# One hybrid attention and convolution trunk: normalized operands made in staggered pairs, and the rest of the gated branch handed out along the last projection

## The chip, the cores and the metric

The kernel runs on one core of a Trainium2 chip. The metric is the device time of one execution in microseconds (us). Engines are named as the profile names them: PE is TensorE, DVE is VectorE, ACT is ScalarE, POOL is GpSimd and SP is SyncE, which issues the DMAs. Every engine works through its own queue in order and waits on semaphores that the others raise.

## The reference, cut to what matters

A sequence of 256 rows of width 2048 runs through two layers and a final RMSNorm, all in float32:

```
hn = rmsnorm(x, norm_g[0])                     # layer 0: forgetting attention, 16 heads of 128
q, k, v, gate, f = split(hn @ fox_w_in)
c = cumsum(log_sigmoid(f + b_f))
p = softmax(q k^T * scale + c_q - c_k, causal)
h = x + ((p v) * silu(gate)) @ fox_w_out

hn = rmsnorm(h, norm_g[1])                     # layer 1: causal Conformer convolution
a, b, gate = split(hn @ conv_w_in + b_in)
u = causal depthwise conv(a * sigmoid(b), 31 taps) + dw_b
y = silu(layernorm(u)) * silu(gate)
out = rmsnorm(h + y @ conv_w_out, final_norm_g)
```

## The kernel before

**Matmuls in three passes.** Every float32 operand is cut in two fp32r numbers: an upper half (the value copied to fp32r by ScalarE, line L100) and a lower half (the value minus its upper half, line L101, on VectorE or GpSimd as the code says). A product is upper x upper, upper x lower, lower x upper. Weights come from HBM in 1 MB tiles (`raw`, three buffers), are cut into `hi` and `lo` (three buffers each), and TensorE takes 48 matmuls of 256 columns from a tile (24 of 512 columns in the value projection and in the last one). A new `hi` can be written when TensorE is through with the tile three before it.

**Order.** TensorE's order is written out by hand. Behind it runs a counter, `now`: a k-row of a 512-wide tile is one step (12 matmuls of 256 columns). `at(n, f)` issues f once the counter has moved on by n, in front of the next k-row (`step`). `line` with `put` is a second list, for VectorE's long work in the convolution: each entry has a length in steps, and entries are issued as the counter passes the sum of the lengths. In layer 0 the tile framework chooses the order on ScalarE, VectorE and GpSimd by the place in the program at which an instruction is issued; from L710 to the first quarter of the last projection the order on these three is also the order of the program.

**Forget sums.** In the first head group the forget gate's log is made on GpSimd in small operations (L494 to L516) into `lfn`. `forget_sums`, issued by `at(18.5, ...)` in L654, sums it along the sequence by two matmuls (`pc`, L524); ScalarE copies the result (`chi`, L527), VectorE builds `cc` (L528 to L531), and GpSimd multiplies `cc` by a head's selector into `la` and `rbh` (L558 to L561). A head's score needs them in its last two matmuls (L566, L567).

**Layer 1.** The first two blocks of 128 channels (b and a of each) are projected from the unnormalized h, and the norm's row scale is applied to the result (`scaled`, L919 to L922). All later blocks use normalized operands `nh` and `nl`, which `normed` (L785) makes for two k-rows at a time: VectorE multiplies h by the row scales into a PSUM tile `n` (L789), ScalarE makes the upper half `nh` (L281), VectorE the lower half `nl` (L282), row after row. Two pairs are put on the line by `norm1_rows`, six more by block 0 (L926), ahead of that block's convolution. Then VectorE runs 31 taps per channel (L814). After the first channel block `mean_shift` (L847) takes a mean by two matmuls on TensorE from its result `dall`; it is issued 12 steps after block 1. At the end of each later pair of channels ScalarE and GpSimd add up sums (L866 to L871).

**The gated branch.** After the LayerNorm, `gated` (L982) makes the normalized, silu'd pair of channels in PSUM, and `gated2` (L994) multiplies it by the gate `sg` and cuts it into the halves `y1a` (channels 0 to 7 of 16) or `y1b` (8 to 15). `y1b` has the place of `nh` in memory, so it cannot be written before the last gate projection has read `nh`. L1014 to L1018 issue the last four pairs at one place ahead of the last projection, whose first quarter (`po`, L244 to L246) takes `y1b` from its ninth k-row on. The weights of that quarter are four tiles from `feed_tiles` (L688), here called c0 to c3, with lower halves from GpSimd in two pieces each; the next quarter's tiles are here called d0 to d3.

Of the kernel before, what the change touches and what calls it, by code (L numbers as in the profile page):

```python
# [8 lines left out]
F32 = mybir.dt.float32  # L9
F32R = mybir.dt.float32r  # L10
AF = mybir.ActivationFunctionType
ALU = mybir.AluOpType

P = 128
D = 2048
S = 256
# [18 lines left out]
def tile_hybrid_trunk(  # L35
# [112 lines left out]
    def feed_tiles(wv, c0, width, engs, order=None):  # L148

        n = KT * width // 2048  # L150
        first = len(feed["specs"])
        feed["specs"] += [(wv, c0, width, (order or range(n))[g], engs) for g in range(n)]
        return first
# [22 lines left out]
    def at(step, fn):  # L176
        agenda.append((now[0] + step, fn))
        agenda.sort(key=lambda e: e[0])
# [438 lines left out]
    for pos, hg in enumerate(ORDER):  # L617

        kT = [
            ph.tile([P, 4, n], dt, name=f"k{i}_{hg}", tag=f"k{i}", bufs=1)  # L620
            for i, (n, dt) in enumerate(((S, F32R), (S, F32R), (P, F32)))
        ]
        qT = [
            ph.tile([P, 4, P], dt, name=f"q{i}_{hg}", tag=f"q{i}", bufs=1) for i, dt in enumerate((F32R, F32R, F32))
        ]
        ps = k_banks if pos == 0 else proj_t(w_fin, D + hg * 512, 512, tiles(ah), tiles(al), VE)

        def qk_evict(dst, ps, scale):
            for b in range(2):
                bs = slice(2 * b, 2 * b + 2)  # L630
                pv = ps[b].rearrange("p (a t) -> p a t", a=2)
                e = ph.tile([P, 2, P], F32, tag="ge", name=f"e{n_stream[0]}_{b}")
                for m, part in enumerate((dst[2][:, bs, :], e)):
                    ts = slice(m * P, (m + 1) * P)
                    nc.vector.scalar_tensor_tensor(
                        part, pv[:, :, ts], scale, rb[:, :, ts].broadcast_to([P, 2, P]), op0=ALU.mult, op1=ALU.mult
                    )
                if dst is kT:
                    for m, part in enumerate((dst[2][:, bs, :], e)):
                        ts = slice(m * P, (m + 1) * P)  # L640
                        split(kT[0][:, bs, ts], kT[1][:, bs, ts], part, nc.gpsimd)
                else:
                    split(qT[0][:, bs, :], qT[1][:, bs, :], e, nc.gpsimd)

        if pos == 0:
            at(8, lambda: row_scales(r0, rb[:, 0, :], "l0"))
            at(11, lambda: qk_evict(kT, k_banks, 1.0))
        else:
            qk_evict(kT, ps, 1.0)
        ps = proj_t(w_fin, hg * 512, 512, tiles(ah), tiles(al), VE, 4 if pos == 0 else 1, made=() if pos else q_made)  # L650
        qk_evict(qT, ps, -float(P) ** -0.5)
        sil = gate_group(hg)
        if pos == 0:
            at(18.5, forget_sums)  # L654
        vN = [
            ph.tile([P, 512], dt, tag=f"v{i}", name=f"v{i}_{hg}", bufs=1) for i, dt in enumerate((F32R, F32R, F32))
        ]
        ps = [psj.tile([P, 512], F32, tag="pj", name=f"pv{hg}_{m}") for m in range(2)]
        for kt, hv, lv in stream(w_fin, 2 * D + hg * 512, 512, VE):
            for m in range(2):  # L660
                products_n(ps[m], kt, hv, lv, tiles(ah), tiles(al), m, kt == 0, kt == KT - 1)
        nc.scalar.activation(vN[0], ps[0], AF.Copy, scale=r0[:, 0:1])
        nc.vector.scalar_tensor_tensor(
            vN[1], ps[0], r0[:, 0:1], vN[0].bitcast(F32), op0=ALU.mult, op1=ALU.subtract
        )
        nc.scalar.activation(vN[2], ps[1], AF.Copy, scale=r0[:, 1:2])
        dist, t0 = 3 if pos < 3 else 2, 0 if pos else 6
        for j in range(4):
            attend(4 * hg + j, qT, kT, vN, sil, t0 + dist * j, t0 + dist * j + 5, t0 + dist * j + 8)
# [15 lines left out]
        a_first[c0] = feed_tiles(w_cin, c0, width, GE if c0 == P else engs)  # L685
    for c in range(4):
        g_first[c] = feed_tiles(w_cin, 2 * D + c * 512, 512, GE)
    cout0 = feed_tiles(w_cout, 0, 512, GE * 2)  # L688

    def residual_add(n, b, ps):  # L690
        kp = slice(4 * n + 2 * b, 4 * n + 2 * b + 2)
# [86 lines left out]
    def norm1_rows(r1):  # L778
        rows = bank_rows(kept_bank("rbk"), 0, r1, "l1")
        put(0.3, lambda: nc.vector.tensor_copy(rb1, rows))  # L780
        for kp in range(2):
            put(0.96, lambda kp=kp: normed(kp, rows))
        kept["rows"] = rows

    def normed(kp, rows):  # L785

        t = bank(f"n{kp}").rearrange("p (a t) -> p a t", a=2)
        ks = slice(2 * kp, 2 * kp + 2)
        nc.vector.tensor_tensor(t, hT[:, ks, :], rows.broadcast_to([P, 2, S]), op=ALU.mult)  # L789
        for i in range(2):  # L790
            split_act(2 * kp + i, 1, nh, nl, t[:, i, :])

    negs = ph.tile([P, S], F32, name="negs", bufs=1)
    accd = ph.tile([P, 2, S], F32, name="accd", bufs=1)
# [98 lines left out]
    def conv_block(c0, width):  # L893
        ct, n = c0 // P, width // P
        normal = ct >= 2
        h, l = (nh, nl) if normal else (ah, al)
        pb = proj_t(w_cin, D + c0, width, tiles(h), tiles(l), None, first=b_first[c0])[0]
        sig = ph.tile([P, 2, S], F32, tag="sig", name=f"sig{ct}", bufs=2)
        if normal:

            at(0.4, lambda: [sigmoid(ct + i, sig[:, i, :], pb[:, i * S : (i + 1) * S]) for i in range(n)])
        pa = proj_t(w_cin, c0, width, tiles(h), tiles(l), None, first=a_first[c0])[0]

        def start():
            bks = [gated_input(ct + i, pa[:, i * S : (i + 1) * S], sig[:, i, :]) for i in range(n)]

            rest = line[:]
            line.clear()
            if n == 1:
                conv_alone(ct, bks[0])  # L910
            else:
                conv_pair(ct, bks)
            line[4:4] = [e for e in rest if e in sums]
            line.extend(e for e in rest if e not in sums)

        if not normal:
            rows = rb1[:, 0, :]

            def scaled():  # L919
                nc.vector.tensor_tensor(sig[:, 0, :], pb[:, 0:S], rows, op=ALU.mult)  # L920
                nc.vector.tensor_tensor(pa[:, 0:S], pa[:, 0:S], rows, op=ALU.mult)
                sigmoid(ct, sig[:, 0, :], sig[:, 0, :])  # L922

            if ct == 0:
                put(2 * HALF, scaled)
                for kp in range(2, KT // 2):  # L926
                    put(0.96, lambda kp=kp: normed(kp, kept["rows"]))
                put(HALF, start)
            else:

                line.insert(min(4, len(line)), (2 * HALF, scaled))
                put(HALF, start)
            return
        put(2 * HALF, start)
# [77 lines left out]
        pump(True)  # L1012
        agenda.pop(0)[1]()
    yb = big.tile([P, 2, HK, S], F32R, tag="B1", name="y1b")  # L1014
    for cp in (4, 5, 6, 7):
        if cp == 7:
            gated(7)
        gated2(cp)  # L1018

    def yh(kt):  # L1020
        return (ya if kt < HK else yb)[:, 0, kt % HK, :]
# [125 lines left out]
```

## Time and profile before

| | us |
|---|---|
| median of 3 runs (lowest, highest) | 897.37 (897.13, 897.63) |
| profiled execution, its own time | 897.78 |
| its span (first to last instruction) | 895.8 |
| PE busy | 876.0 (98%) |
| DVE, ACT, POOL busy | 566.9, 421.8, 381.5 |
| mean granted clock of PE | 0.993 |

The span runs from the first to the last instruction of the profiled execution; the other 1.98 us of its time lie around it. Matmuls overlap, so a busy share of 98% says that PE seldom stands, not that it could do no more. The granted clock is a share of 2.4 GHz; PE runs at that or at half of it.

### The profile page before, as it was taken

Reading aid. Unit: us, or ns where it says so; the run is one execution under the profiler, and the core shown is the slowest. Engines: PE = TensorE matmul, PEld = TensorE weight load, DVE = VectorE, ACT = ScalarE, POOL = GpSimd, SP = SyncE. Lnnn points to the kernel's source line nnn. Section 1 sums busy time; section 2 is a strip of 40 time slices with the busy share of each in tenths; the row PEclk is TensorE's granted clock in tenths of the full one; section 3 lists DMA queues with packets and bytes.
Section 4 is the critical chain, followed back from the end, with each engine's and each line's share of the span. In section 5 each row is a group of like instructions: output and inputs, shape, how many; then the busy total and the mean of one; then the engine's idle time right before and its main releaser. Section 6 shows DMA issues by size and latency. Waiting matters only on the chain.

```text
span 895.8 us, 15928 instructions
## 1 busy us (share of the span) xinstructions
PE 876.0 (98%) x6652; PEld 845.7 (94%) x6652; DVE 566.9 (63%) x1035; ACT 421.8 (47%) x558; POOL 381.5 (43%) x237
## 2 busy tenths in 40 slices
PE   9999999999999999999999988999999999999996
PEld 9999899989999999989999978999999999988886
DVE  5764455446544564446656559999999993628641
ACT  5743355345434553356444463444443355756531
POOL 4130954103410231103100248799798998755110
PEclk9999999999999999999999998999999999999998
DMA  9887987976577998954455446445555556456522
GB/s 290 231 236 152 181 155 142 181 194 180 141 187 171 173 161 171 184 198 160 149 189 152 142 142 199 164 158 186 189 188 188 188 168 208 145 187 232 178 109 94
DMA packets 99499, 157.71 MB, mean 176 GB/s; under 512 B 2676, under 2 KB 40676, under 8 KB 99300
## 3 DMA queue, kind: packets, MB, share of 16 engines
q1 hardware_dynamic: 99092, 155.63, 64.3%
q8 instruction: 52, 0.85, 0.4%
q10 hardware_dynamic: 336, 1.07, 0.3%
q14 instruction: 19, 0.16, 0.0%
HBM read 154.59 MB, written 2.10 MB: 175 GB/s over the span
## 4 chain that ended last, share of the span: by engine, by line
PE 89%; DVE 3%; POOL 3%; ACT 2%; issue 2%; POOLq 0%; DVEq 0%; ACTq 0%
PE pt L216 68%; PE po L246 3%; PE po L245 3%; PE po L244 3%; PE pv L245 2%; PE pv L246 2%; PE pv L244 2%; DVE acc L814 1%; ACT hi L100 1%; DVE nl L282 1%; ACT nh L281 1%; PE sc L564 1%; POOL fg L500 1%; POOL fg L502 1%; PE warm L326 1%
## 5 line engine op out<-in xcount | busy, mean ns | idle before, releaser
L100 ACT ACTIVATE hi<-raw 128x2048 fp32r<-128x2048 f32 (+2 forms) x185 | 270.5, 1485 | 307.5 <-PE pt L216 196.8
L101 DVE TENSOR_TENSOR lo<-raw,hi 128x2048 fp32r<-128x2048 f32 (+1 forms) x132 | 217.6, 1673 | 186.5 <-ACT hi L100 186.3
L101 POOL TENSOR_TENSOR lo<-raw,hi 128x2048 fp32r<-128x2048 f32 (+1 forms) x53 | 227.9, 4313 | 61.0 <-ACT hi L100 61.0
L216 PE MATMUL pt<-ah,hi 128*128 128x256 f32 x768 | 219.6, 286 | 0.0
L216 PE MATMUL pt<-ah,lo 128*128 128x256 f32 x768 | 217.3, 283 | 0.0
L216 PE MATMUL pt<-al,hi 128*128 128x256 f32 x768 | 217.3, 283 | 0.0
L216 PE MATMUL pt<-nh,lo 128*128 128x256 f32 x704 | 200.5, 285 | 4.1 <-POOL lo L101 4.1
L216 PE MATMUL pt<-nh,hi 128*128 128x256 f32 x704 | 201.0, 286 | 0.2 <-ACT hi L100 0.2
L216 PE MATMUL pt<-nl,hi 128*128 128x256 f32 x704 | 200.3, 285 | 0.0
L814 DVE SCALAR_TENSOR_TENSOR acc<-u,dwT,acc 128x256 f32<-128x256 f32 x478 | 188.3, 474 | 0.0
L216 PEld LDWEIGHTS pt<-al,hi 128*128 128x128 f32 x768 | 147.4, 192 | 0.1
L216 PEld LDWEIGHTS pt<-ah,hi 128*128 128x128 f32 x768 | 147.3, 192 | 0.1
L216 PEld LDWEIGHTS pt<-ah,lo 128*128 128x128 f32 x768 | 147.3, 192 | 0.0
L216 PEld LDWEIGHTS pt<-nh,lo 128*128 128x128 f32 x704 | 136.4, 194 | 4.3 <-POOL lo L101 4.3
L216 PEld LDWEIGHTS pt<-nh,hi 128*128 128x128 f32 x704 | 136.5, 194 | 0.5 <-ACT hi L100 0.4
L216 PEld LDWEIGHTS pt<-nl,hi 128*128 128x128 f32 x704 | 136.4, 194 | 0.1
L216 PE MATMUL pt<-yh,hi 128*128 128x256 f32 x256 | 73.3, 286 | 0.0
L216 PE MATMUL pt<-yl,hi 128*128 128x256 f32 x256 | 72.5, 283 | 0.6 <-POOL yl L101 0.6
L216 PE MATMUL pt<-yh,lo 128*128 128x256 f32 x256 | 72.4, 283 | 0.0
L558 POOL CAST la<-ones 64x256 fp32r<-64x256 f32 x16 | 8.5, 529 | 136.0 <-PE sc L567 135.9
L244 PE MATMUL pv<-hi,ah 128*128 128x512 f32 x128 | 50.0, 390 | 0.0
L216 PEld LDWEIGHTS pt<-yl,hi 128*128 128x128 f32 x256 | 49.1, 192 | 0.8 <-POOL yl L101 0.8
(260 smaller groups left out, 1221.1 us busy)
## 6 DMA issues: line engine op xcount, KB each, us to landing
raw<-in_fox_w_in_dram SPq DMA_DIRECT2D x56, 1024.0 KB, 7.6
raw<-in_conv_w_in_dram SPq DMA_DIRECT2D x48, 1024.0 KB, 5.2
raw<-in_fox_w_out_dram SPq DMA_DIRECT2D x16, 1024.0 KB, 5.1
raw<-in_conv_w_out_dram SPq DMA_DIRECT2D x16, 1024.0 KB, 5.1
raw<-in_fox_w_in_dram SPq DMA_DIRECT2D x4, 1056.0 KB, 7.3
rawk<-in_fox_w_in_dram SPq DMA_DIRECT2D x4, 512.0 KB, 10.9
xn<-in_x_dram SPq DMA_DIRECT2D x3, 512.0 KB, 11.2
rawk<-in_fox_w_in_dram SPq DMA_DIRECT2D x4, 256.0 KB, 5.5
```

The costliest lines, as they stand in the source:

```text
L100: nc.scalar.activation(dst_hi, src, AF.Copy)
L101: lo_eng.tensor_tensor(dst_lo, src, dst_hi.bitcast(F32), op=ALU.subtract)
L216: nc.tensor.matmul(ps[nt // 2][:, (nt % 2) * S : (nt % 2 + 1) * S], w[:, nt * P : (nt + 1) * P], a(kt), start=(kt == 0 and i == 0 and nt % ...
L244: nc.tensor.matmul(ps, ah(kt)[:, ms], hv, start=first, stop=False)
L245: nc.tensor.matmul(ps, al(kt)[:, ms], hv, start=False, stop=False)
L246: nc.tensor.matmul(ps, ah(kt)[:, ms], lv, start=False, stop=last)
L281: nc.scalar.activation(hi_t[:, kt, :], src, AF.Copy, scale=gcol)
L282: nc.vector.scalar_tensor_tensor(lo_t[:, kt, :], src, gcol, hi_t[:, kt, :].bitcast(F32), op0=ALU.mult, op1=ALU.subtract)
L326: nc.tensor.matmul(warm[:, 0:P], ones, ones, start=True, stop=True)
L500: g.tensor_tensor(e, base, e, op=ALU.pow)
L502: g.tensor_tensor(s2, s2, neg1, op=ALU.pow)
L814: nc.vector.scalar_tensor_tensor(acc, src, w, acc, op0=ALU.mult, op1=ALU.add)
```

## The change

- `forget_sums` is issued one step later (19.5 instead of 18.5).
- `normed` takes a pair in two calls: one makes `n` and both `nh` of pair kp, and the next one, after the `n` and `nh` of pair kp + 1, makes both `nl` of pair kp. There are nine calls instead of eight, three of them ahead of block 0's own.
- The lower halves of c0 to c3 come from VectorE instead of GpSimd, in two pieces as before.
- In front of the last projection the third tile's halves are issued first (`feed_make(cout0 + 2)`), and the last four pairs of the gated branch are issued at steps 0.5, 1.5, 2.5 (`gated2` 4 to 6), 3.5 (`gated` 7) and 6 (`gated2` 7) of it.

```diff
@@ -651,7 +651,7 @@
         qk_evict(qT, ps, -float(P) ** -0.5)
         sil = gate_group(hg)
         if pos == 0:
-            at(18.5, forget_sums)
+            at(19.5, forget_sums)
         vN = [
             ph.tile([P, 512], dt, tag=f"v{i}", name=f"v{i}_{hg}", bufs=1) for i, dt in enumerate((F32R, F32R, F32))
         ]
@@ -685,7 +685,7 @@
         a_first[c0] = feed_tiles(w_cin, c0, width, GE if c0 == P else engs)
     for c in range(4):
         g_first[c] = feed_tiles(w_cin, 2 * D + c * 512, 512, GE)
-    cout0 = feed_tiles(w_cout, 0, 512, GE * 2)
+    cout0 = feed_tiles(w_cout, 0, 512, VE * 2)
 
     def residual_add(n, b, ps):
         kp = slice(4 * n + 2 * b, 4 * n + 2 * b + 2)
@@ -778,17 +778,27 @@
     def norm1_rows(r1):
         rows = bank_rows(kept_bank("rbk"), 0, r1, "l1")
         put(0.3, lambda: nc.vector.tensor_copy(rb1, rows))
-        for kp in range(2):
-            put(0.96, lambda kp=kp: normed(kp, rows))
         kept["rows"] = rows
-
-    def normed(kp, rows):
-
-        t = bank(f"n{kp}").rearrange("p (a t) -> p a t", a=2)
-        ks = slice(2 * kp, 2 * kp + 2)
-        nc.vector.tensor_tensor(t, hT[:, ks, :], rows.broadcast_to([P, 2, S]), op=ALU.mult)
-        for i in range(2):
-            split_act(2 * kp + i, 1, nh, nl, t[:, i, :])
+        for kp in range(3):
+            put(0.96, lambda kp=kp: normed(kp))
+
+    def normed(kp):
+
+        if kp < KT // 2:
+            t = kept[kp] = bank(f"n{kp}").rearrange("p (a t) -> p a t", a=2)
+            nc.vector.tensor_tensor(
+                t, hT[:, 2 * kp : 2 * kp + 2, :], kept["rows"].broadcast_to([P, 2, S]), op=ALU.mult
+            )
+            for i in range(2):
+                kt = 2 * kp + i
+                nc.scalar.activation(nh[:, kt, :], t[:, i, :], AF.Copy, scale=gT[:, KT + kt : KT + kt + 1])
+        if kp:
+            for i in range(2):
+                kt = 2 * kp - 2 + i
+                nc.vector.scalar_tensor_tensor(
+                    nl[:, kt, :], kept[kp - 1][:, i, :], gT[:, KT + kt : KT + kt + 1], nh[:, kt, :].bitcast(F32),
+                    op0=ALU.mult, op1=ALU.subtract,
+                )
 
     negs = ph.tile([P, S], F32, name="negs", bufs=1)
     accd = ph.tile([P, 2, S], F32, name="accd", bufs=1)
@@ -923,8 +933,8 @@
 
             if ct == 0:
                 put(2 * HALF, scaled)
-                for kp in range(2, KT // 2):
-                    put(0.96, lambda kp=kp: normed(kp, kept["rows"]))
+                for kp in range(3, KT // 2 + 1):
+                    put(0.96, lambda kp=kp: normed(kp))
                 put(HALF, start)
             else:
 
@@ -1012,10 +1022,11 @@
         pump(True)
         agenda.pop(0)[1]()
     yb = big.tile([P, 2, HK, S], F32R, tag="B1", name="y1b")
-    for cp in (4, 5, 6, 7):
-        if cp == 7:
-            gated(7)
-        gated2(cp)
+    feed_make(cout0 + 2)
+    for i, cp in enumerate((4, 5, 6)):
+        at(0.5 + i, lambda cp=cp: gated2(cp))
+    at(3.5, lambda: gated(7))
+    at(6, lambda: gated2(7))
 
     def yh(kt):
         return (ya if kt < HK else yb)[:, 0, kt % HK, :]
```

The names in the rows below are the program's tiles with a buffer number. On VectorE, where the normalized operands are made: `n` is the product of a pair, `nl` its lower halves, `dwT` the taps' weights, `sig` and `pt` block 0's scaling. Before, in the first rows from `n`:

```order
L789 TENSOR_TENSOR n_5465<-hT,rbk 128x512
L282 SCALAR_TENSOR_TENSOR nl_5350<-n_5465,gT,nh_5349 128x256 x2
L762 COPY dwT<-pd 128x496
L789 TENSOR_TENSOR n_5489<-hT,rbk 128x512
L282 SCALAR_TENSOR_TENSOR nl_5350<-n_5489,gT,nh_5349 128x256 x2
L920 TENSOR_TENSOR sig_5419<-pt_0_5355,rb_5336 128x256
L921 TENSOR_TENSOR pt_0_5420<-pt_0_5420,rb_5336 128x256
L789 TENSOR_TENSOR n_5520<-hT,rbk 128x512
```

Here each pair's `nl` follows its own `n`. The same place of VectorE now:

```order
L789 TENSOR_TENSOR n_5465<-hT,rbk 128x512
L762 COPY dwT<-pd 128x496
L789 TENSOR_TENSOR n_5487<-hT,rbk 128x512
L798 SCALAR_TENSOR_TENSOR nl_5350<-n_5465,gT,nh_5349 128x256 x2
L789 TENSOR_TENSOR n_5509<-hT,rbk 128x512
L798 SCALAR_TENSOR_TENSOR nl_5350<-n_5487,gT,nh_5349 128x256 x2
L930 TENSOR_TENSOR sig_5419<-pt_0_5355,rb_5336 128x256
L931 TENSOR_TENSOR pt_0_5420<-pt_0_5420,rb_5336 128x256
L789 TENSOR_TENSOR n_5536<-hT,rbk 128x512
```

Each pair's `nl` now stands behind the next pair's `n`. On ScalarE and then on VectorE, around the forget sums (`hi_1458` and `lo_1459` are the halves of the second k projection's fourth tile, `hi_1370` and `lo_1371` those of its third):

```order
 L100 ACTIVATE hi_1370<-raw_1368 128x2048
 L666 ACTIVATE v_3_1053<-pv_1_1055,r_l_499 128x512
+L100 ACTIVATE hi_1458<-raw_1456 128x2048
 L527 ACTIVATE chi<-pc 128x256
-L100 ACTIVATE hi_1458<-raw_1456 128x2048
 L580 ACT_TABLE_LOAD
```

The upper half now stands ahead of `chi`. VectorE at the same place:

```order
 L101 TENSOR_TENSOR lo_1371<-raw_1368,hi_1370 128x2048
+L101 TENSOR_TENSOR lo_1459<-raw_1456,hi_1458 128x2048
 L528 COPY cc<-chi 128x256
 L531 TENSOR_TENSOR cc<-pc,chi 32x256 x2
-L101 TENSOR_TENSOR lo_1459<-raw_1456,hi_1458 128x2048
 L574 ISA e_1333,nm_1334<-sc_1326,cmask 128x256
```

The lower half now stands ahead of `cc`. On ScalarE, from the last gate projection's silu (`sg`) into the last projection: `hi_8834` and `hi_8866` are c2 and c3, `hi_8969` and `hi_9017` are d0 and d1, `t_8815` is the last pair. Before:

```order
L942 ACTIVATE sg<-pt_1_8543,par 128x256 x2
L100 ACTIVATE y1b<-t_8587 128x512
L100 ACTIVATE y1b<-t_8626 128x512
L100 ACTIVATE y1b<-t_8659 128x512
L990 ACTIVATE t_8815<-t_8815,par 128x256 x2
L100 ACTIVATE y1b<-t_8815 128x512
L100 ACTIVATE hi_8834<-raw_8832 128x1024 x2
L100 ACTIVATE hi_8866<-raw_8864 128x1024 x2
L100 ACTIVATE hi_8969<-raw_8967 128x512 x4
L100 ACTIVATE hi_9017<-raw_9015 128x512 x4
```

All four `y1b` stand ahead of c2, c3, d0 and d1. Now (`hi_8808` and `hi_8863` are c2 and c3, `t_8852` is the last pair):

```order
L952 ACTIVATE sg<-pt_1_8534,par 128x256 x2
L100 ACTIVATE hi_8808<-raw_8806 128x1024 x2
L100 ACTIVATE y1b<-t_8599 128x512
L100 ACTIVATE y1b<-t_8638 128x512
L100 ACTIVATE y1b<-t_8671 128x512
L1000 ACTIVATE t_8852<-t_8852,par 128x256 x2
L100 ACTIVATE hi_8863<-raw_8861 128x1024 x2
L100 ACTIVATE hi_8969<-raw_8967 128x512 x4
L100 ACTIVATE hi_9017<-raw_9015 128x512
L100 ACTIVATE y1b<-t_8852 128x512
L100 ACTIVATE hi_9017<-raw_9015 128x512 x3
```

The third tile now stands ahead of the gated pairs, the fourth ahead of the last pair's `y1b`, and that `y1b` behind d0 and one piece of d1.

## Rows read from the trace of the kernel before

**Rows 1.** Who waited for whom, TensorE over the whole span: total, times, longest

```profile
PE pt L216 <- POOL lo L101: 4.1, 1, 4.1
PE pm L847 <- DVE dall L838: 3.5, 1, 3.5
...
PE lnb L775 <- ACT dg_mr L774: 0.3, 1, 0.3
```

**Rows 2.** TensorE in time: start, duration (us), line, operation, idle before <- releaser

```profile
525.69 0.28 PE L216 MATMUL pt<-nh,hi 128*128 128x256 f32 x1
525.81 0.28 PE L216 MATMUL pt<-nl,hi 128*128 128x256 f32 x1
...
536.39 0.58 PE L216 MATMUL pt<-nh,lo 128*128 128x256 f32 x1 [4.09 <-POOL lo L101]
...
552.71 0.96 PE L847 MATMUL pm<-dall,ones 128*128 128x256 f32 x2 [3.52 <-DVE dall L838]
```

**Rows 3.** Stretches: busy us of PE, PEld, DVE, ACT, POOL; granted clock, DMA

```profile
553.00:556.50 3.50, 3.50 (x17) 3.37 (x16) 3.50 (x10) 0.10 (x1) 3.50 (x1) 0.52 0.93 299
...
800.00:850.00 50.00, 48.28 (x223) 39.29 (x222) 32.85 (x38) 30.36 (x54) 16.16 (x8) 1.00 0.58 195
```

**Rows 4.** Groups, 504 to 560 us: busy, mean ns | idle before, releaser

```profile
L282 DVE SCALAR_TENSOR_TENSOR nl<-n,gT,nh 128x256 fp32r<-128x256 f32 x16 | 7.7, 484 | 11.0 <-ACT nh L281 11.0
L281 ACT ACTIVATE nh<-n,gT 128x256 fp32r<-128x256 f32 x16 | 7.6, 473 | 12.8 <-DVE n L789 8.3 <-DVE nl L282 4.5
L789 DVE TENSOR_TENSOR n<-hT,rbk 128x512 f32<-128x512 f32 x8 | 5.5, 685 | 0.0
```

**Rows 5.** Timeline of VectorE in the same stretch

```profile
511.43 0.69 DVE L789 TENSOR_TENSOR n<-hT,rbk 128x512 f32<-128x512 f32 x1
...
514.15 0.67 DVE L762 COPY dwT<-pd 128x496 f32<-128x496 f32 x1
...
536.31 0.08 DVE L801 MEMSET u<- 128x30 f32 x1
...
540.76 9.09 DVE L814 SCALAR_TENSOR_TENSOR acc<-u,dwT,acc 128x256 f32<-128x256 f32 x23
```

**Rows 6.** Timeline of ScalarE and of GpSimd in the same stretch

```profile
518.78 1.28 ACT L808 ACT_TABLE_LOAD   x1
...
529.84 1.90 ACT L100 ACTIVATE hi<-raw 128x2048 fp32r<-128x2048 f32 x1
...
531.82 4.51 POOL L101 TENSOR_TENSOR lo<-raw,hi 128x2048 fp32r<-128x2048 f32 x1 [8.35 <-ACT hi L100]
```

**Rows 7.** Timeline of four engines around the forget sums

```profile
111.51 1.13 PE L524 MATMUL pc<-tri,lfn 128*128 128x256 f32 x4 [0.80 <-POOL lfn L516]
...
117.29 0.36 PE L566 MATMUL sc<-rbh,la 128*128 128x256 f32 x1
...
113.98 1.91 ACT L100 ACTIVATE hi<-raw 128x2048 fp32r<-128x2048 f32 x1 [0.92 <-PE pt L216]
...
108.33 2.29 DVE L101 TENSOR_TENSOR lo<-raw,hi 128x2048 fp32r<-128x2048 f32 x1 [1.05 <-ACT hi L100]
113.09 0.29 DVE L528 COPY cc<-chi 128x256 f32<-128x256 f32 x1 [2.47 <-ACT chi L527]
...
114.98 0.95 POOL L559 TENSOR_SCALAR la<-cc,sel 64x256 fp32r<-64x256 f32 x2
```

**Rows 8.** Timeline of four engines into the last projection

```profile
806.80 0.50 PE L246 MATMUL po<-lo,y1b 128*128 128x512 f32 x1 [1.72 <-POOL lo L101]
...
794.84 0.69 DVE L101 TENSOR_TENSOR y1b<-t,y1b 128x512 fp32r<-128x512 f32 x1 [11.04 <-ACT y1b L100]
...
792.75 1.57 ACT L942 ACTIVATE sg<-pt,par 128x256 f32<-128x256 f32 x4 [3.10 <-PE pt L216]
...
804.38 10.35 POOL L101 TENSOR_TENSOR lo<-raw,hi 128x1024 fp32r<-128x1024 f32 x4 [9.44 <-ACT hi L100]
```

**Rows 9.** Timeline of ScalarE at a pair's end

```profile
641.12 0.51 ACT L866 ACTIVATE dall<-acc,par 128x256 f32<-128x256 f32 x1 [3.70 <-DVE acc L814]
```

## The prediction

> **What bounds the kernel now.** I read the engines' busy shares first (TensorE 98%), so time can only come from the places where TensorE stands or runs at its lower clock. The list of who waited for whom gives them [rows 1]: 4.1 us for a lower half from GpSimd, 3.5 us for `dall` from VectorE, 0.3 us for the LayerNorm's rows; two more stand in the timelines, 0.80 us for the forget gate's `lfn` [rows 7] and 1.72 us for a lower half in the last projection [rows 8]. All the rest of the span TensorE is at work. The first two lie in one stage, where the normalized operands are made, so I read that stage next, engine by engine.
>
> The reader is to see a chain there. TensorE's matmuls start 0.12 us apart [rows 2]. The 50th after 525.69 is the first to need the lower half of block 2's second weight tile; it could start at 525.69 + 50 x 0.12 = 531.7 and starts at 536.39. That lower half took GpSimd 4.51 us from 531.82, because ScalarE wrote the upper half only from 529.84 [rows 6]. ScalarE was not busy: its queue held that tile behind `nh` of pair 5, and it waited 12.8 us in all for VectorE between the `nh` [rows 4]. VectorE waited 11.0 us for `nh` in turn [rows 4]. The two engines pass each pair back and forth. For the same reason VectorE reaches the convolution only at 536.31 [rows 5], `dall` is late, and `mean_shift`, the 145th matmul, which could start at 525.69 + 144 x 0.12 = 543.0, starts at 552.71 [rows 2]. After it the granted clock is 0.52 for 3.5 us [rows 3]: the engine fell to its lower level, 1.2 GHz, behind a wait of 3.52 us, and that costs 3.5 x 0.48 = 1.7 us more.
>
> **Staggered pairs.** The work is the same: eight `n`, sixteen `nh`, sixteen `nl`. What goes is VectorE's wait, since `nh` of pair kp is made while VectorE makes `n` of pair kp + 1. VectorE's sum from 511.43 to the convolution, now 536.31 - 511.43 = 24.9 us: `n` 5.5 and `nl` 7.7 busy [rows 4], `dwT` 0.67 [rows 5], block 0's two scalings about 0.8 (an estimate: the shape is half of `n`'s), together 14.7. Instructions in a run overlap: 23 taps of `nl`'s shape take 9.09 us, 0.395 each [rows 5], against 0.484 alone [rows 4], so 27 instructions save up to 2.4. Waits that stay: `dwT` now comes before its transposes have landed, about 0.8; and ScalarE has other work between the `nh`, a table load of 1.28 [rows 6], a sigmoid of some 0.5 and two weight tiles of 1.90, of which VectorE's lead over ScalarE covers part; I take 2.0 of these 5.6. Bounds: 12.3 with no waits at all, 14.7 + 0.8 + 5.6 = 21.1 with no overlap and nothing covered. I take 14.7 - 1.7 + 0.8 + 2.0 = 15.8, so the convolution starts at 527.2, 9.1 us earlier. 15.8 is nearer the busy sum, because VectorE runs ahead of ScalarE in all pairs but the two beside ScalarE's other work.
>
> Then what is late next? ScalarE gets to the second tile right behind `nh` of pair 5, at about 522.7 by the same walk, GpSimd has its lower half 1.9 + 4.5 us later at 529.2, and TensorE asks for it at 531.7: 2.5 us of cover, and a miss costs what goes beyond it. `dall` lies on VectorE behind a fixed run of taps, so it moves by the same 9.1: `mean_shift` at 543.6, where TensorE arrives at 543.0. It waits 0.6 us, which VectorE now sets, and behind so short a wait I expect the full clock. Gain: 552.71 - 543.6 = 9.1, and the 1.7 of clock: **10.8 us**. From the bounds of the walk (12.3: `mean_shift` bound by TensorE itself, gain 11.4; 21.1: start at 532.5, gain 3.8, the clock lost again) the gain lies between 3.8 and 11.4.
>
> **Forget sums one step later.** The wait of 0.80 us goes: twelve matmuls now stand ahead of `pc`. But the later place also puts the fourth tile's halves ahead of `chi` on ScalarE and ahead of `cc` on VectorE. That upper half waits for TensorE to finish the tile three before, which these twelve matmuls do; they no longer stand behind `pc` (0.80 + 1.13 us), so it starts at 113.98 - 1.93 = 112.05 instead of 113.98 and ends at 113.96 [rows 7]. `chi` fits behind it, but VectorE first makes the lower half, 2.29 us [rows 7], to 116.25. `cc` started at 113.09, now at 116.25: 3.2 us later. The first `la` was there at 114.98 + 0.48 = 115.46, now at 118.6. TensorE asks for it at 117.29 - 0.80 = 116.5. So a wait of **2.1 us** takes the place of 0.80: **+1.3 us**. Queued behind `cc` on VectorE are the same head's maxima, which need that very score. Bounds: -0.8 (no wait) to +3.0 (half a lower half more, and the clock).
>
> **LayerNorm rows.** The statistics and the rows stand one step later on TensorE, 12 x 0.12 = 1.4 us, more than the 0.3 they are waited for [rows 1]: **-0.3 us**. The gated pairs begin about a microsecond later; VectorE stood 11.04 us between them before [rows 8], so nothing follows.
>
> **Last projection.** Before, c2's upper half stood behind all four pairs on ScalarE, and GpSimd began its lower half at 804.38, four pieces in 10.35 us [rows 8]; TensorE waited 1.72 us [rows 8]. Now c0 and c1 lie in the 11.04 us in which VectorE stood: four pieces of half 2.29, 4.6 us. c2 follows `sg`, which ends at 792.75 + 1.57 = 794.3 [rows 8]: two upper pieces of 1.0, lower done at 797.5. From there a pair takes 0.69 for the product, about 0.6 on ScalarE (an estimate, a quarter of a tile's 1.91 and a start), 0.69 for the lower half [rows 7, 8]: pairs 4, 5, 6 at 799.5, 801.5, 803.5. TensorE enters at about 793.5 and, as the ninth k-row's lower half was due at 806.80 - 1.72 = 805.1, takes 1.4 us per k-row: pair 4 is needed at 804.6, pair 5 at 807.4, pair 6 at 810.2, all covered by over 5 us. Pair 7: products to 804.9, two silus to 806, c3's upper half to 808.0, its lower half to 809.3 (needed at 810.2), the gate's product to 810.0, d0 and one piece of d1 on ScalarE to 810.7, `y1b` to 811.3, its lower half to 812.0; needed at 812.9. The whole **1.7 us** goes, with 0.9 us of cover at c3 and at pair 7; a miss costs its own length, at most some 2 us. GpSimd loses eight pieces of 2.6 us, which nobody else waits for. On SP the loads of c3 and d0 to d2 now wait for VectorE, which is through with c2 at 797.5 where GpSimd ended c2 at 809.6; the final gain's load (`fx`) moves behind d1 and d2 and behind pair 7's product. Its first user is GpSimd's scaling of the output, on which no matmul waits. So I cost that at nothing; without that cover it would be as much as `fx` is later.
>
> **Sum** against the profiled execution: 897.78 - 10.8 + 1.3 - 0.3 - 1.7 = 886.3. The median shown is 0.41 below the profiled time, so **885.9 us**.
>
> **Rivals.** (a) *The pairs shrink less.* For it: ScalarE's other work falls among the `nh`, and each pair's wait counts both halves of `nh`. Against it: rows 4 have VectorE's work at half the stage. At a start of 530 `mean_shift` waits 3.4 us and the clock falls again: 885.9 + 2.8 + 1.7 = 890.4. (b) *The new wait at `la` brings the lower clock:* 885.9 + 1.7 = 887.6. For it: 3.52 us of waiting brought it. Against it: the stretch that holds the 1.72 us wait has the clock at 1.00 [rows 3, 8], and 2.1 is nearer to that. The Trainium skill (TensorE: Matmul & The Clock Gate, "What's actually happening") has the half-rate clock as the default, from which activity releases the engine; by that page any new wait speaks for (b), and no row here has a wait between 1.72 and 3.52. (c) *No wait at `la`*, if VectorE's lower half met a free slot earlier: 885.9 - 2.1 = 883.8. (d) *Pair 7 or c3 misses* in the last projection: up to 2 us, 887.9. (e) *Slower than before:* TensorE gains 10.8 and VectorE 9.1, so through the convolution TensorE runs 1.7 us further ahead of the taps. At a pair's end ScalarE stands until the taps are done, 3.70 us at the longest [rows 9], with the next weight tile queued behind it; that becomes 5.4. A tile has 2 x 48 x 0.12 = 11.5 us from its buffer's release to its use and needs 1.9 + 4.5 [rows 6], so 5.1 are spare; from there on each microsecond is TensorE's. If all six pair ends lost 2.1 us, the time would be 898.5. Against it: part of each wait lies before the buffer is free, and the longest of six was 3.70. (f) *The change does nothing to the stage*, since the next tile's load sets it: then only the last projection gains, 897.4 + 1.3 - 2.0 = 896.7. Against it: VectorE's and ScalarE's waits name each other, not a DMA.
>
> **How the numbers follow.** Forecast 0.60 (own range 884.8 to 887.2), (a) 0.10, (b) 0.07, (c) 0.08, (d) 0.09, (e) 0.03, (f) 0.03. A range of 883.7 to 889.5 takes in the forecast, (b), (c), (d) and half of (a). What a measurement of this kernel can tell from no change is about 0.2%, 1.8 us; only (e) is slower by that, and (f) lies inside: faster 0.94, same 0.03, slower 0.03.
>
> **What the profile after would show.** Right: between the `n` VectorE has almost no wait for `nh`; its convolution starts about 15.8 us after the first `n`; no TensorE wait on GpSimd in that stage, a short one at `mean_shift` and clock 1.00 there; a new wait of about 2.1 us in the first head's score for `la`; none in the last projection. Wrong: a `mean_shift` wait of 3 us or more with the clock at half (a), waits for weight tiles at every pair's end (e), or `y1b` as a releaser in the last projection (d).

## The result and the profile after

| | median of the runs, us | profiled execution, us | its span, us |
|---|---|---|---|
| before | 897.50 (897.13 to 900.42, 4 runs) | 897.78 | 895.8 |
| after | 885.25 (885.10 to 886.27, 4 runs) | 885.23 | 883.4 |

The ratio is 0.9859, 95% interval 0.9837 to 0.9881: faster by 1.4%. Forecast were 885.9 us and, for the profiled execution, 886.3.

Where it came from is read by setting the start of the same TensorE instruction in both traces side by side, from one profiled execution of each:

| TensorE reaches | before, us | after, us | ahead, us |
|---|---|---|---|
| the first forget-gate matmul | 63.06 | 62.91 | 0.15 |
| the row sums (L724) | 506.40 | 507.62 | -1.22 |
| block 2's first matmul | 525.69 | 526.90 | -1.21 |
| `mean_shift` | 552.71 | 544.39 | 8.32 |
| the LayerNorm's second rows | 760.98 | 752.56 | 8.42 (9.86 at equal place: they stand 1.44 later) |
| the first residual rows in the last projection | 814.65 | 802.65 | 12.00 |
| the last matmul | 888.04 | 876.04 | 12.00 |
| the end of the span | 895.8 | 883.4 | 12.4 |

So the forget sums cost 1.22 + 0.15 = 1.37 us, the stage of the normalized operands gave 9.86 + 1.21 = 11.07, the last projection 12.00 - 9.86 = 2.14, and 0.15 and 0.4 lie at the program's two ends. The list of who waited for whom, TensorE after:

```profile
PE sc L566 <- POOL la L559: 2.2, 1, 2.2
PE warm L326 <- POOL ones L80: 1.1, 1, 1.1
PE pt L216 <- POOL yl L101: 0.6, 1, 0.6
...
PE lnb L775 <- ACT dg_mr L774: 0.3, 1, 0.3
```

The 4.1 and 3.5 us of [rows 1] are gone, and so is the 1.72 us of [rows 8]; the new wait is `la`. The timeline of TensorE, with the instructions that answer to [rows 2] and [rows 7]:

```profile
111.83 1.03 PE L524 MATMUL pc<-tri,lfn 128*128 128x256 f32 x4
...
118.47 0.39 PE L566 MATMUL sc<-rbh,la 128*128 128x256 f32 x1 [2.15 <-POOL la L559]
...
526.90 0.28 PE L216 MATMUL pt<-nh,hi 128*128 128x256 f32 x1
...
544.39 0.67 PE L857 MATMUL pm<-dall,ones 128*128 128x256 f32 x2
```

`mean_shift` comes 17.49 us behind block 2's first matmul; 144 x 0.12 = 17.28 would be no wait at all, 27.02 it was. The stretches that answer to [rows 3], with the granted clock third from the end: behind the wait for `la`, around `mean_shift`, and in the last projection.

```profile
119.40:122.70 3.30, 3.30 (x30) 3.30 (x29) 1.06 (x5) 1.88 (x5) 1.65 (x4) 1.00 1.01 184
528.00:552.00 24.00, 23.95 (x199) 23.73 (x198) 23.78 (x63) 10.05 (x10) 20.71 (x5) 1.00 0.54 177
793.00:850.00 57.00, 57.00 (x264) 47.09 (x263) 36.45 (x46) 32.24 (x55) 6.11 (x4) 1.00 0.58 203
```

The groups of 505 to 560 us that answer to [rows 4] (`nl`, `nh`, `n`):

```profile
L798 DVE SCALAR_TENSOR_TENSOR nl<-n,gT,nh 128x256 fp32r<-128x256 f32 x16 | 6.9, 477 | 1.8 <-ACT nh L794 1.7
L794 ACT ACTIVATE nh<-n,gT 128x256 fp32r<-128x256 f32 x16 | 6.5, 475 | 4.0 <-DVE n L789 4.0
L789 DVE TENSOR_TENSOR n<-hT,rbk 128x512 f32<-128x512 f32 x8 | 5.5, 685 | 0.0
```

VectorE's idle time ahead of `nl` fell from 11.0 to 1.8 us, ScalarE's ahead of `nh` from 12.8 to 4.0. The timelines of VectorE, ScalarE and GpSimd in that stage, answering to [rows 5, 6]:

```profile
512.64 0.69 DVE L789 TENSOR_TENSOR n<-hT,rbk 128x512 f32<-128x512 f32 x1
514.15 0.68 DVE L762 COPY dwT<-pd 128x496 f32<-128x496 f32 x1 [0.83 <-PE pd L761]
...
521.41 0.88 DVE L798 SCALAR_TENSOR_TENSOR nl<-n,gT,nh 128x256 fp32r<-128x256 f32 x2 [1.07 <-ACT nh L794]
...
526.33 1.66 DVE L798 SCALAR_TENSOR_TENSOR nl<-n,gT,nh 128x256 fp32r<-128x256 f32 x4 [0.68 <-ACT nh L794]
527.99 0.08 DVE L811 MEMSET u<- 128x30 f32 x1
...
543.83 0.41 DVE L848 TENSOR_TENSOR dall<-acc,u 128x256 f32<-128x256 f32 x1
...
523.65 1.91 ACT L100 ACTIVATE hi<-raw 128x2048 fp32r<-128x2048 f32 x1
...
525.64 13.83 POOL L101 TENSOR_TENSOR lo<-raw,hi 128x2048 fp32r<-128x2048 f32 x3 [2.83 <-ACT hi L100]
```

The convolution starts 527.99 - 512.64 = 15.35 us behind the first `n` (24.9 before). The second tile's lower half, the first of the three in GpSimd's row, ends at 530.3 (a third of 13.83 us behind 525.64); TensorE asks for it at 526.90 + 50 x 0.12 = 532.9.

Around the forget sums and in the last projection, answering to [rows 7, 8]:

```profile
111.91 1.92 ACT L100 ACTIVATE hi<-raw 128x2048 fp32r<-128x2048 f32 x1 [3.19 <-PE pt L216]
113.73 0.36 ACT L527 ACTIVATE chi<-pc 128x256 fp32r<-128x256 f32 x1
...
113.86 2.29 DVE L101 TENSOR_TENSOR lo<-raw,hi 128x2048 fp32r<-128x2048 f32 x1 [3.39 <-ACT hi L100]
116.07 0.28 DVE L528 COPY cc<-chi 128x256 f32<-128x256 f32 x1
...
117.94 0.94 POOL L559 TENSOR_SCALAR la<-cc,sel 64x256 fp32r<-64x256 f32 x2
...
785.51 2.36 DVE L101 TENSOR_TENSOR lo<-raw,hi 128x1024 fp32r<-128x1024 f32 x2 [1.68 <-ACT hi L100]
...
794.46 0.40 PE L244 MATMUL po<-hi,y1b 128*128 128x512 f32 x1
...
801.37 0.69 DVE L101 TENSOR_TENSOR y1b<-t,y1b 128x512 fp32r<-128x512 f32 x1
```

`chi` stands behind the tile's upper half and `cc` behind its lower half, as forecast. c2's lower half is done at 787.9; TensorE comes to the first k-row that takes it, the first of `y1b`, at 794.46.

### The profile page after: what moved, and what is told of

It reads as the page before. It is cut to its first block, busy times and chain, and to the rows that moved or that the text cites. A ratio compares the mean times of both kernels' runs of the same rounds, so it can differ in the third digit from the quotient of the medians.

```text
span 883.4 us, 15933 instructions
## 1 busy us (share of the span) xinstructions
PE 871.9 (99%) x6652; PEld 842.4 (95%) x6652; DVE 569.4 (64%) x1043; ACT 420.6 (48%) x558; POOL 363.4 (41%) x229
## 4 chain that ended last, share of the span: by engine, by line
PE 95%; issue 1%; DMA 1%; ACT 1%; POOL 1%; DVE 0%; SPq 0%; POOLq 0%; DVEq 0%
PE pt L216 72%; PE pv L244 3%; PE pv L245 3%; PE pv L246 3%; PE po L246 3%; PE po L244 3%; PE po L245 3%; DMA rawk<-in_fox_w_in_dram 1%; PE sc L564 1%; PE ptr L593 1%; PE po L609 1%; ACT hi L100 0%; PE sc L565 0%; PE po L610 0%; PE hr L1086 0%
## 5 line engine op out<-in xcount | busy, mean ns | idle before, releaser
L101 DVE TENSOR_TENSOR lo<-raw,hi 128x2048 fp32r<-128x2048 f32 (+2 forms) x140 | 221.4, 1607 | 187.6 <-ACT hi L100 187.3
L101 POOL TENSOR_TENSOR lo<-raw,hi 128x2048 fp32r<-128x2048 f32 x45 | 208.1, 4641 | 42.7 <-ACT hi L100 42.7
```

The costliest lines, as they stand in the source:

```text
L101: lo_eng.tensor_tensor(dst_lo, src, dst_hi.bitcast(F32), op=ALU.subtract)
```

## The experiments

The first weights land at slightly different times in each execution, so that the first forget-gate matmul came between 62.6 and 64.8 us in the profiled runs, whatever the kernel; the medians, which are those of all runs, carry that spread. The column "stretch" leaves it out: it is the time from that matmul (the first `pf`) to the start of the last one, in the one profiled execution of each kernel.

| kernel | median, us | before beside it, us | ratio, 95% interval | stretch, us |
|---|---|---|---|---|
| before | | | | 824.98 |
| after | 885.25 | 897.50 | 0.9837 to 0.9881 | 813.13 |
| e1 sums back | 884.49 | 897.15 | 0.9843 to 0.9874 | 811.77 |
| e2 stagger alone | 886.47 | 897.15 | 0.9875 to 0.9911 | 813.98 |
| e3 last projection alone | 894.35 | 897.15 | 0.9953 to 0.9981 | 821.21 |
| e4 tile early | 897.03 | 897.15 | 0.9988 to 1.0008 | 824.91 |
| e5 sums mid-row | 884.23 | 897.54 | 0.9835 to 0.9864 | 812.11 |
| e6 sums later still | 886.73 | 897.54 | 0.9862 to 0.9892 | 814.61 |
| e7 halves on GpSimd | 886.35 | 897.54 | 0.9857 to 0.9887 | 813.11 |
| e8 old order, VectorE | 887.16 | 897.54 | 0.9866 to 0.9899 | 814.24 |
| e10 mid-row and more | 886.11 | 897.42 | 0.9844 to 0.9892 | 814.55 |
| e11 grouped | 893.86 | 897.42 | 0.9938 to 0.9970 | 822.36 |
| e12 after again | 887.23 | 897.42 | 0.9858 to 0.9902 | 814.60 |
| e13 no wait for la | 882.95 | 897.55 | 0.9830 to 0.9856 | 810.80 |

**The parts.** e1 puts one part back; e2 and e3 each do one part alone, on the kernel before.

```
e1, on the changed kernel:  -            at(19.5, forget_sums)
                            +            at(18.5, forget_sums)
e2, on the kernel before:   norm1_rows, normed and the two loops over kp as in the change, nothing else
e3, on the kernel before:   cout0 = VE * 2, feed_make(cout0 + 2) and the at(...) of the pairs, nothing else
```

> The changed kernel with the forget sums back at their old step. Theory: the later step trades a wait of 0.80 us for one of 2.15 us, because the fourth tile's lower half (2.29 us on VectorE) then stands ahead of cc. So the wait for la goes, the 0.80 us for lfn comes back, and the time is 885.25 - 1.35 = 883.9 us. Rival: the wait for la has another source (the order of the scores); then it stays at about 2 us beside the 0.80, and the time is about 886.0 us.

> The kernel before with the staggered pairs alone. Theory: this part is worth the two waits of 4.1 + 0.2 and 3.5 us and two stretches of half clock of about 1.7 us each, 11.1 us in all: 897.5 - 11.1 = 886.4 us. The waits of 0.80 us (lfn) and of 1.7 + 0.4 us (the last projection) stay, and the LayerNorm's rows stand one step later and are waited for 0.3 us all the same. Rival: a part of the gain needs the other edits (less than 9 us here, 888.5 us or more).

> The kernel before with the edit of the last projection alone. Theory: 1.72 + 0.36 us of waiting for lower halves go and nothing else moves: 897.5 - 2.1 = 895.4 us, with the stage of the normalized operands as it was (4.1 and 3.5 us). Rival: the wait there was set by the weight transfers and comes back elsewhere in the projection: 897.5 us.

e1: 1.36 us less over the stretch than after, the 0.8 us for `lfn` back, none for `la`: as the theory said. (Its profiled run came 1.9 us late to the first forget-gate matmul; two of its four runs took 883.6 and 883.7.) e2: 11.00 us less than before. e3: 3.77 less, not 2.1. Its last projection gave 2.21; the other 1.54 lie behind `mean_shift`, where this run waited 2.86 us and kept the full clock:

```profile
552.85 0.67 PE L847 MATMUL pm<-dall,ones 128*128 128x256 f32 x2 [2.86 <-DVE dall L838]
...
553.00:556.50 3.50, 3.50 (x29) 3.45 (x30) 3.50 (x11) 0.06 (x1) 3.37 (x1) 1.00 0.87 284
```

In the same stretch of [rows 3] the clock was 0.52, with 17 matmuls for these 29. The edit changes nothing as early as that, so these 1.54 us are luck and not a gain of it. Around the 4.1 us wait this run stood at the lower level for longer (0.50 from 536.5 to 541 us, where before had the full clock again from 539.3 us on), which cost nothing, since `mean_shift` waits for `dall` in any case. The two parts that shorten and the one that lengthens add up to the whole: -11.00 - 2.21 + 1.36 = -11.85, and the change gave 813.13 - 824.98 = -11.85. e3's median is 2.8 us below before; which of its other runs fell to the lower clock behind `mean_shift` is not known.

**Is it the tile or the convolution?** e4 makes only the second tile of block 2 early.

```
                 for kp in range(2, KT // 2):
+                    if kp == 4:
+                        put(0, lambda: feed_make(len(feed["made"])))
                     put(0.96, lambda kp=kp: normed(kp, kept["rows"]))
```

> The kernel before with only the second weight tile of block 2 made two pairs earlier on ScalarE; the pairs stay unstaggered. Theory: that VectorE reaches its convolution late is what costs; the first wait alone is worth nothing. TensorE no longer waits 4.1 us for the lower half, arrives at mean_shift at about 543.0 and stands there 9.7 us instead of 3.5, for VectorE starts its convolution at 536.3 as before: 897.5 us, within 0.5. Rival: the lower half is half of the matter; then 4.3 us of waiting and 1.7 us of clock go: 891.5 us.

The time is the theory's (ratio 0.9998), but the wait did not go to `mean_shift`. TensorE in its timeline:

```profile
542.07 0.39 PE L216 MATMUL pt<-nh,lo 128*128 128x256 f32 x1 [4.11 <-POOL lo L101]
...
552.53 0.80 PE L847 MATMUL pm<-dall,ones 128*128 128x256 f32 x2 [3.20 <-DVE dall L838]
```

The same 4.1 us stand one tile later: the third tile's upper half was next in ScalarE's queue, behind `nh` of the last pair, at 535.50. `mean_shift` waited about as before (3.20 us for 3.52). Taking the longest wait from its place was worth nothing, because VectorE's convolution, which sets `dall`, started where it had (536.13, before 536.31). Whether `mean_shift` would have taken over the whole wait, as the theory had it, this run does not show.

**Stagger or only fewer round trips?** e11 keeps each pair together, with both `nh` ahead of both `nl`.

```
-        if kp:
             for i in range(2):
-                kt = 2 * kp - 2 + i
+                kt = 2 * kp + i
```

> The changed kernel with the pairs no longer staggered: each pair's two nh and then its two nl follow its own n, so that VectorE waits once for a pair and not twice as before the change. Theory: a pair then takes VectorE about 2.05 us (n, 0.54 of waiting, two nl) against 2.66 before and 1.4 staggered; the convolution starts some 20 us behind the first n, 4.6 later than in the changed kernel, mean_shift waits about 4.6 us and the clock falls behind it: 885.3 + 4.6 + 1.7 = 891.5 us. Rival: the double wait was the whole matter, and the grouping alone is as good as the stagger: 885.3 to 886 us.

```profile
525.93 0.69 DVE L789 TENSOR_TENSOR n<-hT,rbk 128x512 f32<-128x512 f32 x1
527.53 0.88 DVE L797 SCALAR_TENSOR_TENSOR nl<-n,gT,nh 128x256 fp32r<-128x256 f32 x2 [0.91 <-ACT nh L794]
528.32 0.69 DVE L789 TENSOR_TENSOR n<-hT,rbk 128x512 f32<-128x512 f32 x1
```

The rival falls. In VectorE's timeline a pair takes 528.32 - 525.93 = 2.39 us (forecast 2.05: the wait is 0.91, not 0.54, since the two `nl` start only when both `nh` are done), against 1.38 in the changed kernel (524.97 - 523.59, `n` to `n`). The convolution starts 535.72 - 514.95 = 20.8 us behind the first `n` (forecast some 20), 5.4 later than staggered. From block 2's first matmul to `mean_shift` it is 552.11 - 529.21 = 22.90 us, the same 5.4 more, and the clock falls with the 4.15 us that `mean_shift` waits. The stretch is 822.36, 9.2 above the changed kernel: 5.4 here, 2.35 between `mean_shift` and the statistics (752.24 - 552.11 against 742.17 - 544.39), where the clock is at its lower level for a while, and 1.48 for another such stretch behind `la` (below).

**The forget sums.** e6 moves them on by twelve matmuls, e5 puts them behind the eighth of a row of twelve.

```
e6:  at(20.5, forget_sums)
e5:  at(18.5, lambda: behind.append(forget_sums))
     and in products_t:   if j == 8 and behind: behind.pop()()
```

> The changed kernel with the forget sums yet one step later (twelve matmuls more). Theory: la is late because of the lower half on VectorE, which ends at 116.1 wherever pc stands; so the wait for la stays 2.15 us, within 0.3, and the time is 885.3 us. Rival: la is late because pc is late; then another step adds 1.4 us to the wait, it comes to 3.6 us, and the clock may fall: 886.7 to 888.4 us.

> The changed kernel with the forget sums put in the middle of a row of twelve matmuls: behind the eighth, 0.96 us later than before the change and 0.48 us earlier than after it. ScalarE then takes chi ahead of the fourth tile's upper half again, and VectorE cc ahead of its lower half. Theory: TensorE comes to pc when lfn is there (it was 0.80 us early before), and la is there when it is asked for: neither wait, so 2.15 us less than the changed kernel, 883.1 us, and 0.8 us less than with the sums at their old step. Rival: the two waits are the same wait in two places, and one of 0.8 us or more stays: 883.9 us or more.

e6: the wait is 2.15 us again, to the hundredth, so la's time is set by the lower half on VectorE and not by `pc`. But the stretch is 1.48 us longer, and the median, 886.73, lies in the rival's range for a reason that the rival did not have. The granted clock of the 3.3 us behind the wait, in e6:

```profile
119.40:122.70 3.30, 3.30 (x18) 3.30 (x17) 1.02 (x5) 0.97 (x4) 1.60 (x4) 0.50 0.97 171
```

18 matmuls where the changed kernel made 30: the lower level, 1.2 GHz, behind a wait of the same length. So the changed kernel itself was run again.

> The changed kernel itself, unaltered, beside these on the same chip, so that they can be compared with it and not with the kernel before alone: 885.3 us.

```profile
117.00:119.90 2.90, 0.76 (x7) 0.57 (x5) 1.64 (x4) 0.00 (x0) 1.46 (x4) 1.00 1.00 174
...
120.80:124.10 3.30, 3.30 (x20) 3.30 (x19) 1.09 (x7) 0.99 (x4) 1.68 (x4) 0.58 1.00 176
```

The same program, the same wait of 2.15 us, and here the clock fell: the stretch is 1.47 us longer than in its first profile, and the median of these four runs (885.5 to 888.15) 2 us above that of the first four; beside them the change is worth 10.2 us, where the first runs gave 12.25. The profiled execution is 2.92 us longer than the first: these 1.47, and 1.44 because it came later to the first forget-gate matmul (64.35 for 62.91). Of the six profiles with that wait (after, e6, e7, e8, e11, e12) three have the drop. This wait costs 2.15 us in some executions and 3.6 in others.

e5: the wait for `lfn` is gone, but TensorE still waited 1.04 us for `la`, which its theory had at nothing; the stretch is 1.02 us shorter than after, not 2.15. GpSimd and VectorE there:

```profile
113.59 0.94 POOL L561 TENSOR_SCALAR rbh<-cc,sel 64x256 fp32r<-64x256 f32 x2 [2.02 <-DVE cc L532]
114.62 3.04 POOL L560 TENSOR_SCALAR la<-cc,sel 64x256 fp32r<-64x256 f32 x2
...
114.62 2.32 DVE L101 TENSOR_TENSOR lo<-raw,hi 128x2048 fp32r<-128x2048 f32 x1 [0.68 <-ACT hi L100]
```

The two `la` took 3.04 us together instead of the 0.95 of [rows 7], the first of them 2.59, just while VectorE made a lower half from two inputs. e10 tests that by scaling the first head's `la` and `rbh` on VectorE, ahead of the lower half; e13 is the same without e10's second edit.

```
+        g = nc.gpsimd if firsts else nc.vector
+        firsts.append(hd)
-        nc.gpsimd.tensor_scalar(la[64:128], ...)      and the same for rbh
+        g.tensor_scalar(la[64:128], ...)
e10 only:  LN_ROWS = 7   (was 6)
```

> The kernel with the sums in the middle of a row, and two more edits: the first head's la and rbh are scaled on VectorE instead of GpSimd, and the LayerNorm's rows are asked for one step later (7 for 6) while the statistics stay. Theory: the 1.04 us that the mid-row kernel still waited for la came from GpSimd's two la instructions (3.04 us instead of 0.95) that ran beside VectorE's lower half; on VectorE they stand ahead of it, and the wait is gone; the row wait of 0.27 us goes too, since now the distance from statistics to rows grows. 884.0 - 1.04 - 0.27 = 882.7 us. Rival: la is late through chi and cc, whoever scales it; then 1 us of waiting stays: 883.7 us.

> The mid-row kernel with the first head's la and rbh on VectorE and the LayerNorm's rows at their old step (6). Theory: neither the wait for lfn nor that for la (from the first forget-gate product to the row sums 442.4 us, as in the kernel with the rows a step later, against 444.7 in the changed kernel and 443.7 in the mid-row kernel), and the row wait back at 0.27 us: 884.0 - 1.3 = 882.7 us, with up to 1.5 us more in runs whose first weights land later. Rival: the wait taken away at la comes back as another one before the row sums, and the time is that of the mid-row kernel, 884.0 us.

The wait for `la` is gone in both. e10 lost more elsewhere, by the second edit; its ScalarE, and TensorE with the granted clock behind its wait:

```profile
750.65 1.91 ACT L100 ACTIVATE hi<-raw 128x2048 fp32r<-128x2048 f32 x1 [3.84 <-PE pt L217]
752.47 0.68 ACT L779 ACTIVATE dg_rl<-ident,rl 128x128 f32<-128x128 f32 x2
...
752.91 1.23 PE L780 MATMUL lnb<-dg_rl,ones 128*128 128x128 f32 x4 [2.23 <-ACT dg_rl L779]
...
753.00:756.30 3.30, 3.24 (x14) 2.94 (x15) 0.81 (x2) 0.95 (x3) 3.30 (x1) 0.50 0.81 303
```

One step later, `dg_rl` stands behind a weight tile, and TensorE waited 2.23 us where it had waited 0.27: the trap of the forget sums once more. Behind that wait the clock fell too, and over the stretch e10 is 3.75 us longer than e13. e13, at 882.95 us (882.62 to 883.01), is the fastest of all, 2.33 us shorter than after over the stretch. TensorE's waits in it:

```profile
PE warm L327 <- POOL ones L80: 1.1, 1, 1.1
PE pt L217 <- POOL yl L101: 0.6, 1, 0.6
PE lnb L780 <- ACT dg_mr L779: 0.3, 1, 0.3
```

**Order or engine in the last projection?** On the changed kernel, e7 has `GE * 2` for `VE * 2` at `cout0`; e8 has the loop of the four pairs ahead of the projection again, as before the change.

> The changed kernel with the lower halves of the last projection's first tiles on GpSimd, as before, and the rest handed out along it. Theory: the order alone takes c2's halves out from behind the four pairs; GpSimd makes a piece in 2.6 us where one is used in 2.8 us, so it just keeps up: 885.3 to 885.8 us, with waits of 0.5 us at most. Rival: VectorE is what the gain comes from, and a wait of about 2 us stands in the last projection again: 887.3 us.

> The changed kernel with the four pairs ahead of the last projection as before, but its lower halves on VectorE. Theory: c2's upper half then stands behind the pairs on ScalarE as before, and VectorE gains 2.6 - 1.2 = 1.4 us on its first piece: a wait of 0.3 to 0.7 us where 2.1 stood: 885.6 to 885.9 us. Rival: the order is everything, and 1.7 us or more of waiting come back: 887.0 us.

e7: no wait in the last projection, and the stretch is the changed kernel's to 0.02 us; its rival falls. e8 waits here:

```profile
796.30 0.50 PE L246 MATMUL po<-lo,y1b 128*128 128x512 f32 x1 [0.53 <-DVE lo L101]
```

That is the wait its theory named, but over the stretch it lost 1.1 us: the rest lies in the matmuls around the wait, which start 0.3 to 0.4 us apart instead of 0.23. Its median is at the rival's time, its stretch between the two. So the order alone takes away the 2.1 us, and VectorE alone about 1.0. e7's median is 0.55 us above the end of its theory's range; 0.4 of that lie behind the last matmul (last section), the rest is not settled.

## Why the prediction was right, by its steps

- **Staggered pairs**, forecast 10.8 us, measured 11.07 and 11.00 alone (e2). Of the 11.07, 8.32 + 1.21 = 9.53 lie up to `mean_shift` (forecast 9.1) and 1.54 behind it, where the clock stays up (forecast 1.7). The walk of 15.8 us came out at 15.35: waits for `nh` 1.75 (forecast 2.0), for `dwT` 0.83 (0.8). Those 0.45 us took `mean_shift`'s forecast wait of 0.6 down to 0.2; the clock there is 1.00, as forecast. The clock had also been at 0.50 behind the 4.1 us wait (536 to 539.3 us before), which the prediction did not say; it changes nothing in the sum, since `mean_shift` waited for `dall` in any case. e4 and e11 show the cause: the convolution's start, and the stagger itself.
- **Forget sums**, forecast +1.3, measured +1.37 and 1.36 (e1). The chain was right link by link: `la` forecast for 118.6, there at 118.42. What the step had too simply was "no clock drop": it holds in half of the profiles, so that the first profile had none was luck; the rival (b), given 0.07 and priced at 1.7 us, is what e12's execution did, for 1.47. That any new wait speaks for (b) is more than the runs bear out: waits of 1.04 (e5), 1.06 (e11) and 1.72 us (before) had the full clock behind them. The section of the Trainium skill that spoke for (b) (TensorE: Matmul & The Clock Gate, "What's actually happening") also says that the chip's watch on activity runs free of the kernel's start, so that the same kernel has a different number of matmuls at the lower clock at its start from run to run. The traces show the like in the middle of a kernel: one program with and without the drop, and none behind 2.86 us in e3.
- **LayerNorm rows**, forecast -0.3, measured 0: this step failed. "One step later on TensorE" moved the statistics together with the rows, 10.40 us apart before (750.58 to 760.98) and 10.39 after. The wait belongs to the distance, and 0.27 us stayed. e10 widened the distance and met ScalarE's queue instead.
- **Last projection**, forecast -1.7, measured -2.14: the step left out 0.42 us beside the named 1.72, in the matmuls around the wait, which started 0.33 us apart instead of 0.23. Of the walk, c2's lower half was forecast for 797.5 and pairs 4 to 6 for 799.5, 801.5 and 803.5; less the 9.9 us by which TensorE came earlier to `y1b`, 787.6, 789.6, 791.6 and 793.6. They ended at 787.9, 789.8, 791.8 and 793.8. e7 shows that VectorE's halves were not needed for it.
- **The ends**: 0.15 us at the start and 0.4 at the end were in no term. Between the profiled executions the sum missed by 12.55 - 11.5 = 1.05 us, with the 0.3 of the LayerNorm rows against the rest. The medians are 12.25 us apart in the first runs and 10.2 in e12's, and the forecast of 11.5 lies between: the 0.65 us by which it missed the first median is less than the kernel's own spread.
- **Rival (e)**: ScalarE's longest wait at a pair's end rose from 3.70 to 3.83 us, not to 5.4, and TensorE waited for no weight tile there.

## What to carry to other kernels

Of several waits in one stage, ask which engine sets the last of them: the longest wait, taken from its place by itself, only moved (e4), and all of it went once the engine behind the last wait was freed (e2). A step that is moved in time also changes sides with its neighbours in the queues of other engines: two moves by one step cost 2.15 and 2.23 us for that reason, and in the first case a place eight matmuls on instead of twelve, with two small operations on another engine, had neither wait (e13). A wait on TensorE of a few microseconds is to be priced with the clock behind it, as a range.

## What the runs showed of the hardware that was not expected

- The same wait can bring the lower clock in one execution and not in another: 2.15 us in the same program, three profiles of six with the drop, some 1.5 us each. The waits of 4.09 to 4.11 us for a weight tile (before, e3, e4) had it, as had those of 3.20 (e4), 3.52 (before) and 4.15 us (e11) at `mean_shift` and the one of 2.23 at the LayerNorm's rows (e10); one of 2.86 at `mean_shift` (e3) and one of 1.06 at block 2 (e11) did not.
- A small GpSimd instruction that meets a lower half on VectorE can last until that has ended: the two `la` 3.04 us for 0.95 in e5, and in the changed kernel one step of the forget gate's chain 2.25 us where its like take 0.22:

```profile
102.34 0.25 POOL L507 TENSOR_TENSOR fg<-fg 128x32 f32<-128x32 f32 x1
102.68 2.25 POOL L508 TENSOR_SCALAR fg<-fg 128x32 f32<-128x32 f32 x1
...
102.56 2.29 DVE L101 TENSOR_TENSOR lo<-raw,hi 128x2048 fp32r<-128x2048 f32 x1 [3.10 <-ACT hi L100]
```

  The Trainium skill (SBUF — State Buffer, "SBUF: two separate sides") has the two engines share a pair of ports that one of them holds for a whole instruction, VectorE when it reads two inputs from SBUF while GpSimd reads SBUF too. These rows agree: the step ends at 104.93, just behind the lower half at 104.85. e13 gained 1.3 us over e5 by keeping clear of it.

- From the last matmul's start to the end of the span it is 7.8 us in the kernels whose lower halves of the last projection's first tiles come from GpSimd (before, e2, e4, e7) and 7.4 where they come from VectorE, though the instructions in that time are the same. The 0.4 us lie at GpSimd's last instructions: its last drain starts 0.4 us behind the clearing of the semaphores (895.4 and 895.0 before) instead of 0.1 (883.1 and 883.0 after) and takes 0.18 us instead of 0.03. The former kernels have 19 instruction packets on queue q14, the latter 20 or 21. What links these stays open.
